# Sums of MLP weights in HBM: begun two to a load in attention, fewer per load behind it

## The chip, the cores and the metric

The kernel runs on one core of one Trainium2 chip. The metric is the device time of one execution in microseconds (us), the median of several runs. One profiled execution stands beside the runs; all rows below come from it.

## The reference

One decoder layer over 512 tokens of width 1024, in float32. A pooling mixer and a sparse attention mixer run side by side on the normed input, are merged by sigmoid gates, go through an output projection, and an MLP with squared ReLU follows. Cut to what matters here:

```python
def reference(x, ...):
    h = rms_norm(x, norm_mix)
    proj = h @ w_in
    y_pool = pool_mixer(u, w_pool, pool_scale)
    y_nsa = nsa_mixer(q, kc, vc, ksl, vsl, kwn, vwn, g_nsa, ...)   # 16 heads, rope on q and k
    merged = g_a * (y_pool @ w_proj_pool) + g_b * (y_nsa @ w_proj_nsa)
    x = x + merged @ w_out
    h = rms_norm(x, norm_mlp)
    x = x + jnp.square(jax.nn.relu(h @ w_ff1)) @ w_ff2
    return rms_norm(x, norm_final)
```

## The kernel before

Every float32 product is made of three faster products: a weight tile is loaded as `raw` (128x1024 floats, 512 KB), ScalarE writes its rounded high part `wh` (lines 304 and 350), VectorE or, in attention, GpSimd for half a tile the rest `wl` (306, 352), and TensorE multiplies high by high, high by low and low by high.

The order of the program is: projections of the input (lines 861 to 894, list `P1`), attention (line 1152, 96 slots; a slot is one block of scores), output projection (`fm3`, `tm3`, from line 1304), MLP (line 1551, four chunks of 1024 hidden channels), final norm. In attention a slot's scores are made on TensorE (`score_pe`), cut and summed by VectorE and ScalarE (`smax`, `expo`), multiplied by their weight two slots later on GpSimd (`weight`, line 1078), turned on TensorE five slots later (`turn_pe`, line 1095) and multiplied with the values (`pv`, 1129). Between the slots TensorE fills in the gate projections of the list `FILL2` (13 weights, `gb0` to `gb7`). The first slots wait for the scores of the compressed branch (`cmp_scores`, 959 to 999): VectorE (971 to 985), GpSimd (`cw`, `PC`, lines 987 to 990), TensorE's turn (996).

The MLP uses a fast matrix multiplication with seven products in place of eight, whose weights are partly sums of quarters of `w_ff1` and `w_ff2`. These sums are made by the DMA engines in HBM, without any compute engine, as 44 jobs in a fixed order. A job `S` has two halves: a copy of one quarter into `S`, issued on SyncE (SP) by `make_sum` (line 263), and an addition of another quarter to `S`, an accumulating DMA issued on GpSimd (POOL) by `add_sum` (line 271). An addition waits until its copy has landed. Some jobs copy another sum (`S2<-S1`, `S4<-S2`), so their copies wait, on SP, until that sum's addition has landed.

When a job is begun is decided by `emit_load` (214 to 239): it puts the next weight load on SP (line 233), asks `sums_after(i)` whether a copy follows load number i, and from load 52 on puts an addition on POOL when more than two jobs are begun. In attention the slot loop puts one addition on POOL behind every fourth slot (lines 1174 and 1175). `make_sum` first puts out additions as long as its source is a sum that has not been added to. Loads are numbered by use: 0 to 34 are `P1`, 35 to 47 `FILL2`, 48 to 55 the nsa projection, 56 to 63 the output projection, from 64 on the MLP. Four `raw` buffers (five later) hold loads, so load i goes out when the weight four before it has been split.

SP also issues four 64 KB copies per rope (`rs<-rx`, line 617), which swap the halves of a head; VectorE's first product of that rope (line 619) overwrites `rx` and waits for them. Instructions of one engine run in the order in which the scheduler of the tile framework puts them, from its own estimate of times; SP and POOL are queues like the others, and an instruction that waits holds all behind it.

Of the kernel before, what the change touches and what calls it, by code (L numbers as in the profile page):

```python
# [62 lines left out]
def trunk(ctx: ExitStack, tc: tile.TileContext, A, out):  # L63
# [41 lines left out]
    def add_key(k):  # L105
# [14 lines left out]
        else:  # L120
# [4 lines left out]
    P1 = ("ck ks u0 wk0 wk1 u1 wk2 u2 kw wk3 cv u3 V0 V1 V2 wv0 q0 wv1 ga0 wv2 wpool q1 wv3 ga1 q5 "  # L125
          "ga2 q2 pp0 q6 pp1 q7 pp2 q3 pp3 q4").split()
    FILL2 = "gb0 gb1 gb2 ga3 gb3 ga4 gb4 ga5 gb5 ga6 gb6 ga7 gb7".split()
# [86 lines left out]
    def emit_load():  # L214

        i = st["load"]
        if i >= len(LD):
            return False
        segs = LD[i]
        a = segs[0][0].shape[1]  # L220
        b = sum(s.shape[2] for s, _ in segs)
        assert a * b <= 1024
        if not by_name() or st["kept"] < RAW:
            st["kept"] += by_name()
            t = wp.tile([128, 1024], F32, tag="raw", bufs=RAW, name=f"raw{i}")
        elif spare:
            t = spare.pop(0)
        else:
            return False
        st["load"] += 1  # L230
        v = t[:, :a * b].rearrange("p (a b) -> p a b", a=a)
        for s, o in segs:
            began = nc.sync.dma_start(v[:, :, o:o + s.shape[2]], s)
        raws[i] = (t, a, b)
        if sums_after(i):
            make_sum(began)
        if i >= len(P1) + len(FILL2) + 4 and (len(begun) > 2 or begun and st["sums"] == len(jobs)):
            add_sum()
        return True

    def sums_after(i):

        if i < MLP0:
            return len(P1) + 3 <= i < len(P1) + len(FILL2) + 8
        return i % 3 == 0

    def by_name():

        return st["load"] >= MLP0

    def give_back(*tiles):
        spare.extend(tiles)
        while spare and by_name() and emit_load():
            pass

    def make_sum(load):

        if st["sums"] < len(jobs):
            to, q, _ = jobs[st["sums"]]
            while any(q is jobs[n][0] for n in begun):  # L260
                add_sum()
            with tc.issue_after(load.ins):
                nc.sync.dma_start(to, q)
            begun.append(st["sums"])
            st["sums"] += 1

    def add_sum(behind=None):

        to, _, q = jobs[begun.popleft()]
        with tc.issue_after(behind.ins) if behind else nullcontext():  # L270
            POOL.dma_start(to, q, accum_op=ALU.add)  # L271
# [15 lines left out]
    def group_steps(i):  # L287

        key, at = WL[i]
        if i in PLUS:  # L290
            while st["load"] <= PLUS[i]:
                assert emit_load()
            t = raws.pop(PLUS[i])[0]
            DVE.tensor_tensor(t, t, held[key], op=ALU.add)
            give_back(held.pop(key))
            yield
        elif isinstance(at, str):
            t = held.pop(key)
        else:
            while st["load"] <= at:  # L300
                assert emit_load()
            t = raws.pop(at)[0]
# [248 lines left out]
    def evac0(i, after=None):  # L551
        sl = slice(128 * i, 128 * i + 128)
        for a in range(2):
            ks = slice(4 * a, 4 * a + 4)
            r = ACT.activation(hT[0][:, ks, sl], trs[i][a], AF.Copy)
            with behind(after) if after else nullcontext():
                v = DVE.tensor_tensor(hT[1][:, ks, sl], trs[i][a], hT[0][:, ks, sl].bitcast(F32), op=ALU.subtract)
        return r, v
# [8 lines left out]
    r, _ = evac0(1)  # L567
# [105 lines left out]
    with ExitStack() as c1:  # L673
# [187 lines left out]
        for k in P1[2:]:  # L861
            i = int(k[-1]) if k[-1].isdigit() else None
# [813 lines left out]
```

## Time and profile before

| | us |
|---|---|
| median of 3 runs (791.01 to 793.32) | 792.94 |
| the profiled execution's own time | 793.79 |
| its span, first to last instruction | 792.0 |
| TensorE busy | 774.8 (98%) |
| VectorE busy | 619.3 (78%) |
| ScalarE busy | 488.6 (62%) |
| GpSimd busy | 179.5 (23%) |
| mean granted TensorE clock | 0.996 of full speed |

A difference to the time before is made against the profiled execution's own time, 793.79, which is 0.85 above the median. Busy TensorE means that a matmul was under way by the profile's modelled ends; a wait of a few tenths of a us can hide in it. DMA rows count 16 engines: a share of 1.00 is all of them busy.

### The profile page before, as it was taken

Reading aid. Unit: us, or ns where it says so; the run is one execution under the profiler, and the core shown is the slowest. Engines: PE = TensorE matmul, PEld = TensorE weight load, DVE = VectorE, ACT = ScalarE, POOL = GpSimd, SP = SyncE. Lnnn points to the kernel's source line nnn. Section 1 sums busy time; section 2 is a strip of 40 time slices with the busy share of each in tenths; the row PEclk is TensorE's granted clock in tenths of the full one; section 3 lists DMA queues with packets and bytes.
Section 4 is the critical chain, followed back from the end, with each engine's and each line's share of the span. In section 5 each row is a group of like instructions: output and inputs, shape, how many; then the busy total and the mean of one; then the engine's idle time right before and its main releaser. Section 6 shows DMA issues by size and latency. Waiting matters only on the chain. (4 is left out here: it accounts for less than half of the span.)

```text
span 792.0 us, 12823 instructions
## 1 busy us (share of the span) xinstructions
PE 774.8 (98%) x4541; PEld 674.1 (85%) x4541; DVE 619.3 (78%) x1177; ACT 488.6 (62%) x962; POOL 179.5 (23%) x245
## 2 busy tenths in 40 slices
PE   8999999999999999999999999999999999999995
PEld 6889877888888888988888899879997999789974
DVE  6888666445999888887656489997899789878897
ACT  6756543335988888896334485934783478247745
POOL 4000000025876666673100000111110110110002
PEclk9999999999999999999999999999999999999998
DMA  9554733487753434335956508989998996978552
GB/s 309 134 152 120 198 108 100 127 213 185 135 108 80 99 90 107 80 81 93 346 145 216 130 1 243 327 205 298 260 289 227 281 285 198 279 227 259 165 181 107
DMA packets 116154, 142.33 MB, mean 180 GB/s; under 512 B 5525, under 2 KB 88121, under 8 KB 115898
## 3 DMA queue, kind: packets, MB, share of 16 engines
q1 hardware_dynamic: 97690, 117.72, 45.8%
q0 software_dynamic: 18112, 23.07, 19.2%
q10 hardware_dynamic: 288, 0.72, 0.3%
q8 instruction: 36, 0.59, 0.3%
q14 instruction: 28, 0.23, 0.1%
HBM read 136.77 MB, written 48.23 MB: 234 GB/s over the span
## 5 line engine op out<-in xcount | busy, mean ns | idle before, releaser
L393 PE MATMUL psF<-R,wh 128*128 128x512 f32 x512 | 164.4, 402 | 0.0
L304 ACT ACTIVATE wh<-raw 128x1024 fp32r<-128x1024 f32 x75 | 79.2, 1058 | 85.7 <-PE psB L1515 32.1
L271 POOL DMA_DIRECT2D S<-w_ff x44 | 48.7, 1107 | 360.3 <-DMA S<-w_ff 286.1
L350 ACT ACTIVATE wh<-raw 128x512 fp32r<-128x512 f32 (+1 forms) x100 | 60.3, 620 | 85.3 <-PE psF L393 43.3
L306 DVE TENSOR_TENSOR wl<-raw,wh 128x1024 fp32r<-128x1024 f32 x75 | 92.2, 1231 | 23.4 <-ACT wh L304 23.4
L393 PEld LDWEIGHTS psF<-R,wh 128*128 128x128 f32 x512 | 92.1, 188 | 17.9
L393 PE MATMUL psF<-R,wl 128*128 128x512 f32 x256 | 101.3, 396 | 0.0
L1078 POOL TENSOR_SCALAR P<-P,sm,GT 128x128 f32<-128x128 f32 (+3 forms) x128 | 83.1, 671 | 55.2 <-DVE sm L1068 38.7
L352 DVE TENSOR_TENSOR wl<-raw,wh 128x512 fp32r<-128x512 f32 (+1 forms) x85 | 58.6, 696 | 26.3 <-ACT wh L350 26.2
L1062 ACT ACTIVATE P<-P,sm 128x128 f32<-128x128 f32 (+3 forms) x128 | 71.1, 559 | 9.9 <-DVE sm L1052 9.2
L1052 DVE CUSTOM_DVE_ANT_0 P<-psS,cst 128x128 f32<-128x128 f32 (+3 forms) x128 | 59.7, 483 | 8.4 <-PE psT L1095 5.3
L1398 PE MATMUL psB<-R,wh 128*128 128x256 f32 x352 | 64.1, 282 | 0.0
L304 ACT ACTIVATE w3h<-raw 128x1024 fp32r<-128x1024 f32 x37 | 39.1, 1055 | 36.3 <-PE psB L1398 14.1
L1110 DVE TENSOR_TENSOR PT<-psT,PT 128x512 fp32r<-128x512 f32 (+2 forms) x96 | 56.6, 596 | 3.5 <-ACT PT L1106 2.9
L393 PEld LDWEIGHTS psF<-R,wl 128*128 128x128 f32 x256 | 48.1, 188 | 11.3
L1106 ACT ACTIVATE PT<-psT 128x512 fp32r<-128x512 f32 (+2 forms) x96 | 49.5, 520 | 8.8 <-PE psT L1095 7.8
L1398 PEld LDWEIGHTS psB<-R,wh 128*128 128x128 f32 x352 | 54.3, 189 | 0.5 <-DVE R L1340 0.2
L306 DVE TENSOR_TENSOR w3l<-raw,w3h 128x1024 fp32r<-128x1024 f32 x37 | 45.8, 1238 | 9.2 <-ACT w3h L304 9.2
L1095 PE MATMUL psT<-ident,P 128*128 128x128 f32 x320 | 50.9, 273 | 0.9 <-DVE PT L1110 0.9
L1398 PE MATMUL psB<-R,wl 128*128 128x256 f32 x176 | 49.5, 281 | 0.0
L1095 PEld LDWEIGHTS psT<-ident,P 128*128 128x128 f32 x320 | 39.4, 140 | 9.7 <-issue 1.8
L1129 PE MATMUL psO<-PT,VV 128*128 128x256 f32 x320 | 47.7, 286 | 0.0
(381 smaller groups left out, 2001.8 us busy)
## 6 DMA issues: line engine op xcount, KB each, us to landing
raw<-w_ff SPq DMA_DIRECT2D x54, 512.0 KB, 6.1
S<-w_ff POOLq DMA_DIRECT2D x44, 512.0 KB, 7.5
raw<-S SPq DMA_DIRECT2D x44, 512.0 KB, 5.0
raw<-w_in SPq DMA_DIRECT2D x32, 512.0 KB, 4.1
S<-w_ff SPq DMA_DIRECT2D x32, 512.0 KB, 7.1
S<-S SPq DMA_DIRECT2D x12, 512.0 KB, 5.3
raw<-w_proj_nsa SPq DMA_DIRECT2D x8, 512.0 KB, 4.4
raw<-w_out SPq DMA_DIRECT2D x8, 512.0 KB, 4.5
```

The costliest lines, as they stand in the source:

```text
L304: ACT.activation(h, t, AF.Copy)
L306: DVE.tensor_tensor(l, t, h.bitcast(F32), op=ALU.subtract)
L350: ACT.activation(h[:, sl], t[:, sl], AF.Copy)
L352: eng.tensor_tensor(l[:, sl], t[:, sl], h[:, sl].bitcast(F32), op=ALU.subtract)
L393: PE.matmul(ps, a, b, start=first and j == 0, stop=last and j == n - 1, skip_group_check=True)
L1052: DVE.tensor_tensor_reduce(out=P[:, o:o + n].rearrange("p (a c) -> p a c", c=128), in0=s, in1=m, scale=1.0, scalar=3e38, op0=ALU.add, op1= ...
L1062: last_exp[:] = [ACT.activation(c, c, AF.Exp, bias=sm[:, 0, e:e + 1], scale=-1.0, accum_out=sm[:, 1, e:e + 1])]
L1078: r = POOL.tensor_scalar(P[:, o:o + n], P[:, o:o + n], sm[:, 2, e:e + 1], GT[:, qb, c + e:c + e + 1], op0=ALU.mult, op1=ALU.mult)
L1095: PE.transpose(pt[:, 128 * j:128 * j + 128], P[:, 128 * j:128 * j + 128], ident)
L1106: ACT.activation(dH, src, AF.Copy)
L1110: DVE.tensor_tensor(dL, src, dH.bitcast(F32), op=ALU.subtract)
L1398: PE.matmul(out, w[u][:, k, 128 * f:128 * f + 128], XB[x][v][:, k, :], **kw)
```

## The change

Copies of sums are begun by another count. Between loads 38 and 47 (attention's filler weights) each load is followed by two copies in place of one; between 48 and 55 (the nsa projection) by one at odd loads in place of one at each; from 64 on (MLP) by one at every fourth load in place of every third. Jobs, their order, and all arithmetic stay. By the end of load 55, 24 jobs are begun where it was 18.

```diff
-        if sums_after(i):
+        for _ in range(sums_after(i)):
             make_sum(began)
...
     def sums_after(i):

+        if i < len(P1) + len(FILL2):
+            return 2 * (i >= len(P1) + 3)
         if i < MLP0:
-            return len(P1) + 3 <= i < len(P1) + len(FILL2) + 8
-        return i % 3 == 0
+            return i % 2 * (i < len(P1) + len(FILL2) + 8)
+        return i % 4 == 0
```

Lines behind 243 carry numbers higher by 2 in the changed kernel.

SP, from load 38 to load 43, the end of the projections and the first slots of attention (`raw38` is the buffer of load 38, `S1_100` the sum S1 of layer 1, chunk 0, group 0). Before:

```order
L233 DMA raw38_1563<-w_in 128x8x128
L263 DMA S1_100_69<-w_ff1 512x1x256
L233 DMA raw39_1613<-w_in 128x8x128
L263 DMA S3_100_70<-w_ff1 512x1x256
L617 DMA rs_348<-rx_347 32x512 x4
L233 DMA raw40_1678<-w_in 128x8x128
L263 DMA S1_101_72<-w_ff1 512x1x256
L233 DMA raw41_1717<-w_in 128x8x128
L263 DMA S3_101_73<-w_ff1 512x1x256
L233 DMA raw42_1755<-w_in 128x8x128
L263 DMA S2_100_71<-S1_100_69 16x8192
L233 DMA raw43_1810<-w_in 128x8x128
```

and in the changed kernel:

```order
L233 DMA raw38_1563<-w_in 128x8x128
L265 DMA S1_100_69<-w_ff1 512x1x256
L265 DMA S3_100_70<-w_ff1 512x1x256
L233 DMA raw39_1614<-w_in 128x8x128
L265 DMA S1_101_72<-w_ff1 512x1x256
L265 DMA S3_101_73<-w_ff1 512x1x256
L619 DMA rs_348<-rx_347 32x512 x4
...
L233 DMA raw42_1762<-w_in 128x8x128
L265 DMA S1_201_77<-w_ff2 256x1x512
L265 DMA S3_201_78<-w_ff2 256x1x512
L233 DMA raw43_1817<-w_in 128x8x128
L265 DMA S1_110_79<-w_ff1 512x1x256
```

Four copies stand ahead of the last rope's `rs<-rx` where two stood, and behind load 42 come the copies of S1_201 and S3_201, which were behind loads 46 and 47.

POOL over the same stretch (`cw` and `PC` belong to the compressed branch of the first pair of heads, `P` is the block of a slot, two slots share a row of `sm`). Before:

```order
L271 DMA S1_100_69<-w_ff1 512x1x256
L352 TENSOR_TENSOR wl36_1665<-raw36_1486,wh36_1664 128x512
L352 TENSOR_TENSOR wl37_1703<-raw37_1530,wh37_1702 128x512
L987 TENSOR_TENSOR cw_1653<-cw_1653,c8_1654 128x8x32
L989 TENSOR_SCALAR PC_136<-cw_1653 128x4x64
L990 TENSOR_TENSOR PC_136<-cw_1653,PC_136 128x4x64
L352 TENSOR_TENSOR wl38_1744<-raw38_1563,wh38_1743 128x512
L352 TENSOR_TENSOR wl39_1787<-raw39_1613,wh39_1786 128x512
L1078 TENSOR_SCALAR P_1797<-P_1797,sm_1796,GT_129 128x128 x2
L1078 TENSOR_SCALAR P_1816<-P_1816,sm_1796,GT_129 128x128 x2
L271 DMA S3_100_70<-w_ff1 512x1x256
L1078 TENSOR_SCALAR P_1832<-P_1832,sm_1831,GT_129 128x256 x2
```

and in the changed kernel:

```order
L989 TENSOR_TENSOR cw_1655<-cw_1655,c8_1656 128x8x32
L354 TENSOR_TENSOR wl38_1751<-raw38_1563,wh38_1750 128x512
L991 TENSOR_SCALAR PC_136<-cw_1655 128x4x64
L992 TENSOR_TENSOR PC_136<-cw_1655,PC_136 128x4x64
L354 TENSOR_TENSOR wl39_1794<-raw39_1614,wh39_1793 128x512
L273 DMA S1_201_77<-w_ff2 256x1x512
L273 DMA S3_201_78<-w_ff2 256x1x512
L1080 TENSOR_SCALAR P_1804<-P_1804,sm_1803,GT_129 128x128 x2
L1080 TENSOR_SCALAR P_1824<-P_1824,sm_1803,GT_129 128x128 x2
L273 DMA S3_101_73<-w_ff1 512x1x256
L273 DMA S1_110_79<-w_ff1 512x1x256
L1080 TENSOR_SCALAR P_1840<-P_1840,sm_1839,GT_129 128x256 x2
```

The split of weight 38 now stands between `cw` and `PC`, and the additions to S1_201 and S3_201 stand ahead of the first slots' weights, those to S3_101 and S1_110 ahead of slot 2. On VectorE the first half of the split of weight 38 (line 352) likewise moved ahead of the last step of `cmp_scores` (line 985).

SP in the last third of the MLP, where the sum S2_230 is copied into S4_230. Before:

```order
L263 DMA S2_230_107<-S3_230_106 16x8192
L233 DMA raw64_4838<-S1_221_97 128x1024
L233 DMA raw66_4886<-S3_220_96 128x1024
L233 DMA raw5_4496<-w_ff2 128x2x512
L263 DMA S4_230_108<-S2_230_107 16x8192
```

and in the changed kernel:

```order
L265 DMA S2_230_107<-S3_230_106 16x8192
L233 DMA raw67_4910<-S2_121_94 128x1024
L233 DMA raw66_4900<-w_ff1 128x4x256
L233 DMA raw64_4850<-w_ff1 128x4x256
L233 DMA raw5_4509<-w_ff2 128x2x512
L265 DMA S4_230_108<-S2_230_107 16x8192
```

Four loads stand between a sum's copy and the copy that needs its addition, where three stood; the pair comes six and five loads earlier.

## Rows read from the trace of the kernel before

**Rows 1.** The page, part 1: busy us, share of the span, instructions.

```profile
PE 774.8 (98%) x4541; PEld 674.1 (85%) x4541; DVE 619.3 (78%) x1177; ACT 488.6 (62%) x962; POOL 179.5 (23%) x245
```

**Rows 2.** Windows by stage: us, busy (instructions) by engine, clock, DMA share, GB/s.

```profile
160.00:190.00 30.00, 30.00 (x139) 24.53 (x138) 13.40 (x29) 12.27 (x27) 9.11 (x8) 1.00 0.76 206
190.00:366.00 176.00, 174.01 (x1138) 153.98 (x1137) 156.84 (x500) 153.71 (x423) 117.64 (x169) 1.00 0.48 100
...
480.00:560.00 80.00, 79.20 (x504) 70.85 (x503) 70.06 (x83) 43.92 (x57) 9.06 (x8) 1.00 0.98 279
560.00:640.00 80.00, 80.00 (x514) 72.30 (x513) 68.92 (x81) 47.14 (x63) 8.94 (x8) 1.00 0.96 264
640.00:720.00 80.00, 78.16 (x497) 70.12 (x496) 67.37 (x80) 44.92 (x59) 7.60 (x8) 1.00 0.84 238
```

**Rows 3.** The page, part 3: DMA queue, packets, MB, share of 16 engines' span.

```profile
q1 hardware_dynamic: 97690, 117.72, 45.8%
q0 software_dynamic: 18112, 23.07, 19.2%
```

**Rows 4.** DMA issues at 120 to 160 us: KB each, median us to landing.

```profile
rs<-rx SPq DMA_DIRECT2D x15, 64.0 KB, 2.0
```

**Rows 5.** DMA issues at 160 to 168 us, same columns.

```profile
S<-w_ff SPq DMA_DIRECT2D x2, 512.0 KB, 5.2
S<-w_ff POOLq DMA_DIRECT2D x1, 512.0 KB, 8.5
```

**Rows 6.** Queues (packets, MB, share) and DMA issues at 169 to 172 us.

```profile
q0 software_dynamic: 328, 0.34, 73.3%
q1 hardware_dynamic: 486, 0.47, 44.3%
...
rs<-rx SPq DMA_DIRECT2D x4, 64.0 KB, 5.1
```

**Rows 7.** Timeline of VectorE: start us, us, line, what [idle before, releaser].

```profile
175.88 0.69 DVE L619 TENSOR_TENSOR rx<-rx,cst 128x512 f32<-128x512 f32 x1 [6.16 <-DMA rs<-rx]
...
182.38 0.17 DVE L985 TENSOR_TENSOR c<-c,GT 128x8 f32<-128x8 f32 x1
182.48 0.69 DVE L352 TENSOR_TENSOR wl<-raw,wh 128x512 fp32r<-128x512 f32 x1
```

**Rows 8.** Timeline of GpSimd, from the compressed branch to slot 3.

```profile
166.63 1.34 POOL L271 DMA_DIRECT2D S<-w_ff  x1 [41.05 <-DMA S<-w_ff]
...
182.67 0.98 POOL L987 TENSOR_TENSOR cw<-cw,c 128x256 f32<-128x256 f32 x1 [4.34 <-ACT GB L912]
...
184.23 0.73 POOL L990 TENSOR_TENSOR PC<-cw,PC 128x256 fp32r<-128x256 f32 x1
184.92 1.30 POOL L352 TENSOR_TENSOR wl<-raw,wh 128x512 fp32r<-128x512 f32 x1
...
190.55 1.75 POOL L1078 TENSOR_SCALAR P<-P,sm,GT 128x128 f32<-128x128 f32 x4 [1.01 <-DVE sm L1068]
192.24 1.13 POOL L271 DMA_DIRECT2D S<-w_ff  x1
194.05 2.60 POOL L1078 TENSOR_SCALAR P<-P,sm,GT 128x256 f32<-128x256 f32 x4 [0.68 <-DVE sm L1068]
```

**Rows 9.** Timeline of TensorE: turns of the compressed branch, of slots 2 and 3.

```profile
186.02 0.46 PE L996 MATMUL psT<-identR,PC 128*128 128x128 f32 x4
...
199.82 0.60 PE L1095 MATMUL psT<-ident,P 128*128 128x128 f32 x4
...
200.85 0.60 PE L1095 MATMUL psT<-ident,P 128*128 128x128 f32 x4
```

**Rows 10.** Timeline of SP's queue: the load of weight 42.

```profile
186.25 0.37 SPq L233 DMA_DIRECT2D raw<-w_in  x1
```

**Rows 11.** Groups by line, GpSimd, 190 to 366 us: busy us, mean ns, idle before.

```profile
L1078 POOL TENSOR_SCALAR P<-P,sm,GT 128x128 f32<-128x128 f32 (+3 forms) x126 | 80.7, 663 | 51.1 <-DVE sm L1068 34.6 <-PE psT L1095 9.7 <-PE psF L393 3.4
L271 POOL DMA_DIRECT2D S<-w_ff x13 | 14.4, 1108 | 0.0
```

**Rows 12.** Waits of SP's queue at 640 to 720 us: us in total, times, longest.

```profile
SPq L263 <- DMA S<-w_ff: 25.0, 3, 9.7
```

**Rows 13.** Timeline of SP's queue in the last third of the MLP.

```profile
669.90 0.47 SPq L263 DMA_DIRECT2D S<-S  x1
670.47 0.52 SPq L233 DMA_DIRECT2D raw<-S  x1
```

**Rows 14.** Timeline of ScalarE, the same stretch.

```profile
675.39 1.06 ACT L304 ACTIVATE wh<-raw 128x1024 fp32r<-128x1024 f32 x1 [1.08 <-DMA raw<-S]
...
685.78 1.06 ACT L304 ACTIVATE wh<-raw 128x1024 fp32r<-128x1024 f32 x1 [4.22 <-DMA raw<-w_ff]
```

**Rows 15.** Waits of TensorE at 676 to 690 us: us in total, times, longest.

```profile
PE psB L1515 <- DVE x L1539: 1.8, 1, 1.8
```

## Prediction

> **What bounds the kernel now.** Read the page's busy line first: TensorE is busy 774.8 of 792.0 us, the others 78% and less [rows 1]. So the time is TensorE's work plus what it waits, and all that any change of transfers can win is 17 us, most of it at the two ends. Then the windows by stage [rows 2]: TensorE has no idle time at 160 to 190 us, 2.0 us in attention (190 to 366), and 0.8, 0.0 and 1.8 us in three stretches of the MLP. DMA is the other column to read there: 0.48 of its 16 engines in attention, 0.98, 0.96 and 0.84 in the MLP. The change moves transfers from the crowded stages to the empty one. What it can win is the MLP's 2.6 us of TensorE waits; what it can lose is any cover in a stage where TensorE does not wait now. Third come the timelines of the stretch in which the moved transfers start [rows 5 to 10]: the reader is to see there how little slack lies between a GpSimd result and the TensorE instruction that takes it.
>
> **Price of a transfer.** POOL's queue holds the 44 additions: 19.2% of 792.0 us is 152 us, 3.5 us of all 16 engines for each. SP's queue moves 117.72 MB in 45.8%, 363 us: 3.1 us per MB, 1.6 us for a copy or load of 0.52 MB [rows 3]. A whole job is 5.1 us. Six jobs leave the MLP: some 30 us of the 222 busy DMA us at 480 to 720.
>
> **Step 1: the compressed branch, 0.8 us lost.** TensorE turns `PC` at 186.02, straight behind a matmul, and `PC` is complete at 184.23 + 0.73 = 184.96 [rows 8, 9]: 1.1 us of slack. The changed order puts the split of weight 38 between `cw` and `PC` on GpSimd, 1.30 us [rows 8], and half of the same split, 0.69 less an overlap of 0.1, ahead of line 985 on VectorE, from which `cw` starts [rows 7, 8]. 1.30 + 0.6 - 1.1 = 0.8 us that TensorE waits. In-order TensorE takes the whole stage along. Ends: 0 (the split on VectorE not ready and no later than before) to 1.3.
>
> **Step 2: the last rope, 3.2 us lost.** The chain of step 1 begins on VectorE behind line 619, which already waits 6.16 us for `rs<-rx` [rows 7]. Earlier ropes land in 2.0 us [rows 4], this one in 5.1 [rows 6], 3.1 more, with one addition under way from 166.63 to 175.1 (8.5 us [rows 5]). In the changed kernel S3_100's copy goes out behind S1_100's, lands 5.2 us later [rows 5], at about 167.5, and its addition follows the first at about 168, before the rope's copies go out at 169.5; S1_101's addition follows at about 172. Two more copies stand ahead on SP. Upper end: two additions and two copies in full, 7.0 + 3.2 = 10.2 us. Lower end: 0, if the copies ahead have drained and engines are shared. I take one addition's worth, 3.2, since the one that was in the way cost 3.1: the nearest row. The 619 chain has no other cover: what it loses, TensorE loses at 186.02. Weight 37's split stands right behind it and moved ahead of line 625, so it stays inside its slack.
>
> The Trainium skill, "DMA: Bandwidth & Descriptors", section "Queues, rings and completion order", says that each DMA engine goes round-robin between queues and changes after a packet. By that rule more additions in line would not hold `rs<-rx` longer than one does now, step 2 would be near 0, and the total near that of the first rival. The 5.1 against 2.0 us of the rope speaks against an even share, though not against any.
>
> **Step 3: the first slots' weights, 1.0 us lost.** Load 42 goes out at 186.25 [rows 10]; the copies of S1_201 and S3_201 now follow it, and their additions stand ahead of the weights of slots 0 and 1, which ran at 190.55 [rows 8]. Shifted by steps 1 and 2, less the 1.1 us by which weight 38 is split earlier, they go out near 189 and land 5.2 to 8.5 us later [rows 5], near 196; two additions of 1.1 us [rows 8] end near 197.5. Then come weights of 1.75, S3_101's addition, S1_110's (its copy is behind load 43, landing near 200), and at 201 the 256-wide weights at 0.65 each, split by the 1.30 us split of weight 40: slot 2 done at 202.3, slot 3 at 205. TensorE turns these at 199.82 and 200.85 now [rows 9], shifted by 4.0: 203.8 and 204.9. That is level. Each us by which the copies land later costs one; ends 0 and 4. I take 1.0, because six more transfers than now are in line in that stretch.
>
> **Step 4: the rest of attention, 0.3 us lost.** Eight more additions of 1.1 us run on POOL until the end of attention, 9 us. They stand behind every fourth slot, on copies begun long before, so none waits. Cover: the weights sit idle 51 us ahead of their instructions [rows 11], and they run some 4 us ahead of their turns [rows 8, 9]. If the cover were gone it would be 1.1 us a time; ends 0 and 1.5. On SP the copies S2_110 and S2_111 find their sums added to or wait a few us with nothing urgent behind.
>
> **Step 5: the MLP, 1.8 us won.** The one TensorE wait of size there is 1.8 us on a VectorE addition [rows 15]. Followed back: ScalarE waits 4.22 us for a load of `w_ff`, after 1.08 us for a load of a sum [rows 14], and that load stood on SP at 670.47 behind the copy S4_230<-S2_230, which held the queue 9.7 us for the addition to S2_230 [rows 12, 13]. With four loads between the pair in place of three and fewer additions in line, the hold shrinks at least by the time to one more load, and its place in the chunk changes. I book the whole 1.8. Ends: 2.6 won (all idle time of the three stretches) and 2 lost (a hold in a worse place). What is late next is VectorE, 70.06 of 80 us busy in the first of these stretches [rows 2]; that stays.
>
> **Sum.** 0.8 + 3.2 + 1.0 + 0.3 - 1.8 = 3.5 us more. Against the profiled 793.79 that is 797.3; the median of the runs lies 0.85 lower, so I forecast **796.4 us**, 0.4% slower.
>
> **Rivals.** A measurement tells about 0.3%, 2.4 us, so "the same" is 790.6 to 795.3.
>
> First: even sharing. If a small copy on SP's queue gets its turn whatever is in line on POOL's, step 2 is 0: 0.8 + 1.0 + 0.3 - 1.8 = +0.3, 793.2 us. For it: at 169 to 172 us both queues move packets, POOL's 0.34 and SP's 0.47 MB [rows 6]. The rule above would give this rival. Against: the rope's 5.1 us. It decides if `rs<-rx` lands no later than 176. Chance 0.28.
>
> Second, on the other side: the MLP was held by its DMA, more than the waits show. If the first slots' copies land before 194 (then steps 2 and 3 are covered), and the relief of 30 DMA us takes all 2.6 us of idle time, 792.9 - 2.6 = 790.3 us, faster. For it: 0.98 and 0.96 DMA share in the MLP. Against: TensorE does not wait at all at 560 to 640 with a share of 0.96 [rows 2]. It decides where step 1's 0.8 is covered too, as by line 985 coming early. Chance 0.17.
>
> Third: the change relieves nothing, because SP's holds only move. Then step 5 is 0 and it is 798.2; with a rope at 5 us late, 800. Inside my forecast's side. A forecast of "slower", with this, has 0.55.
>
> **How the numbers follow.** 0.55 for slower (795.3 to about 801), of which a twentieth may end at 795.3 or less: 0.53 slower, 0.30 the same, 0.17 faster. The range must take in the first rival and the edge of the second: from 790.8. Its upper end is steps 1 to 3 at 1.3 + 5 + 3 with step 5 at 1.8: +7.8, 800.7. Steps 2 and 3 at both full ends at once (10.2 and 4) are left out: they overlap, since what delays TensorE gives the weights time.
>
> **What would show it.** Right: TensorE idle ahead of line 996 (998 in the changed kernel) by 2 to 6 us near 186; VectorE's wait for `rs<-rx` near 9 us; POOL idle ahead of the additions to S1_201 and S3_201; DMA share of 480 to 720 lower by about 0.1; SP's longest wait for a sum below 7 us; no TensorE wait of 1.8 near 687. Wrong: `rs<-rx` landing by 176, the turn at 186 on time, or a TensorE wait over 1 us in a new place of the MLP. A time under 791 would say that steps 1 to 3 together cost nothing.

## The result and the profile after

The changed kernel takes **797.6 us** in the median of five runs (797.07 to 800.41) where the kernel before, run beside it, takes 792.94 (791.01 to 793.68): 4.7 us or 0.6% by the two medians. The ratio formed over all of these runs is 1.0075, with a 95% interval of 1.0050 to 1.0101. So the changed kernel is slower, by 0.6 to 0.75%. The profiled execution took 800.19 us with a span of 798.4, at the upper end of the five; 6.4 us of span have to be found against the 792.0 of before.

The page's busy line and its queues stand as they did [rows 1, 3]:

```profile
PE 776.8 (97%) x4541; PEld 674.3 (84%) x4541; DVE 618.4 (77%) x1177; ACT 489.9 (61%) x962; POOL 178.7 (22%) x245
...
q1 hardware_dynamic: 97690, 117.72, 45.9%
q0 software_dynamic: 18112, 23.07, 19.0%
```

Nothing was added to any engine, so the time is waits, and the windows by stage say where [rows 2]:

```profile
160.00:190.00 30.00, 28.73 (x133) 23.25 (x132) 12.22 (x24) 10.95 (x20) 10.06 (x10) 1.00 1.07 280
190.00:366.00 176.00, 172.35 (x1114) 152.43 (x1113) 152.14 (x493) 150.81 (x416) 122.16 (x173) 0.99 0.60 129
480.00:560.00 80.00, 76.75 (x475) 67.65 (x475) 69.16 (x83) 45.27 (x60) 6.65 (x6) 1.00 0.84 239
560.00:640.00 80.00, 80.00 (x515) 72.31 (x514) 69.19 (x81) 46.81 (x61) 6.73 (x6) 1.00 0.87 241
640.00:720.00 80.00, 79.32 (x507) 71.32 (x506) 68.27 (x81) 46.14 (x61) 6.27 (x6) 1.00 0.81 236
```

The transfers moved as the change says: the DMA share falls from 0.98, 0.96, 0.84 to 0.84, 0.87, 0.81 in the MLP and rises from 0.76 to 1.07 at the end of the projections. TensorE now idles 1.3 us there (0 before) and 3.7 us in attention (2.0), and in the MLP the idle time has moved rather than gone: 3.3, 0.0 and 0.7 us in place of 0.8, 0.0 and 1.8.

The timeline of TensorE shows every wait of attention's start (lines behind 243 have numbers higher by 2):

```profile
187.39 0.54 PE L998 MATMUL psT<-identR,PC 128*128 128x128 f32 x4 [1.27 <-POOL PC L992]
...
202.54 0.96 PE L1097 MATMUL psT<-ident,P 128*128 128x128 f32 x4 [1.13 <-POOL P L1080]
...
205.34 0.69 PE L1097 MATMUL psT<-ident,P 128*128 128x128 f32 x2 [1.03 <-POOL P L1080]
...
223.92 0.30 PE L1097 MATMUL psT<-ident,P 128*128 128x128 f32 x1 [0.34 <-DVE PT L1112]
...
480.79 0.39 PE L1400 MATMUL psB<-xT2H,wh 128*128 128x256 f32 x1 [0.64 <-ACT wh L306]
...
762.91 0.73 PE L1517 MATMUL psB<-w3h,yT2H 128*128 128x512 f32 x2 [0.23 <-ACT w3h L306]
```

The last three rows are waits that the kernel before has too, so they serve as marks. In the timeline of TensorE before they stand at

```profile
218.37 0.30 PE L1095 MATMUL psT<-ident,P 128*128 128x128 f32 x1 [0.32 <-DVE PT L1110]
...
475.50 0.39 PE L1398 MATMUL psB<-xT2H,wh 128*128 128x256 f32 x1 [0.65 <-ACT wh L304]
...
756.42 0.73 PE L1515 MATMUL psB<-w3h,yT2H 128*128 128x512 f32 x2 [0.23 <-ACT w3h L304]
```

With the turn of `PC` (186.02 before [rows 9], 187.39 now) that gives the loss by stretch: **1.4 us** up to that turn; from it to the first mark 36.5 us in place of 32.3, **4.2 us**; from there to the second mark 256.9 in place of 257.1, a gain of 0.3; from the second to the third, the MLP, 282.1 in place of 280.9, **1.2 us**; behind it -0.1. The sum is 6.4.

Of the first: VectorE's wait for the rope is 8.39 us, and the split of weight 38 stands between `cw` and `PC`, as the order said [rows 7, 8]:

```profile
178.04 0.69 DVE L621 TENSOR_TENSOR rx<-rx,cst 128x512 f32<-128x512 f32 x1 [8.39 <-DMA rs<-rx]
```

The timeline of GpSimd over the same stretch and on to the first slots:

```profile
184.30 0.62 POOL L989 TENSOR_TENSOR cw<-cw,c 128x256 f32<-128x256 f32 x1 [6.56 <-DVE c L987]
184.88 1.29 POOL L354 TENSOR_TENSOR wl<-raw,wh 128x512 fp32r<-128x512 f32 x1
...
186.62 0.72 POOL L992 TENSOR_TENSOR PC<-cw,PC 128x256 fp32r<-128x256 f32 x1
...
195.64 2.17 POOL L273 DMA_DIRECT2D S<-w_ff  x2 [5.19 <-DMA S<-w_ff]
197.26 2.29 POOL L1080 TENSOR_SCALAR P<-P,sm,GT 128x128 f32<-128x128 f32 x4
198.97 2.93 POOL L273 DMA_DIRECT2D S<-w_ff  x2
```

Of the second: GpSimd stands 5.19 us in front of two additions whose copies have not landed, and the weights of slots 0 and 1, which ran at 190.55 [rows 8], run at 197.26: 6.7 us later, in a stage that is 1.4 us late up to there.

### The profile page after: what moved, and what is told of

Its sections match the earlier page's. It is cut to its first block, busy times and chain, and to the rows that moved or that the text cites. A ratio compares the mean times of both kernels' runs of the same rounds, so it can differ in the third digit from the quotient of the medians.

```text
span 798.4 us, 12822 instructions
## 1 busy us (share of the span) xinstructions
PE 776.8 (97%) x4541; PEld 674.3 (84%) x4541; DVE 618.4 (77%) x1177; ACT 489.9 (61%) x962; POOL 178.7 (22%) x245
## 5 line engine op out<-in xcount | busy, mean ns | idle before, releaser
L273 POOL DMA_DIRECT2D S<-w_ff x44 | 51.8, 1196 | 365.2 <-DMA S<-w_ff 243.0
L1080 POOL TENSOR_SCALAR P<-P,sm,GT 128x128 f32<-128x128 f32 (+3 forms) x128 | 87.2, 792 | 50.0 <-DVE sm L1070 32.5
```

The lines of the kernel that those rows point to most:

```text
L1080: r = POOL.tensor_scalar(P[:, o:o + n], P[:, o:o + n], sm[:, 2, e:e + 1], GT[:, qb, c + e:c + e + 1], op0=ALU.mult, op1=ALU.mult)
```

## Experiments

"Before" ran beside each group of experiments: its median was 791.95, 792.04 and 791.79 us. The expectations name theories: A, or "theory now", is what the traces had suggested by then; B, the steps of the prediction; C, the prediction's first rival. A ratio is to the kernel before; its 95% interval stands in brackets.

**1. The attention part alone.** The changed kernel, with the MLP's count put back:

```diff
-        return i % 4 == 0
+        return i % 3 == 0
```

> Only the attention part of the change: two copies to a load at loads 38 to 47, odd loads at 48 to 55; the MLP begins one behind every third load, as before. Theory A (read from the changed kernel's trace): the start of attention costs about 5.5 us, 1.4 at the turn of PC near 186 and 4.1 at the first slots' turns at 201 to 204, and the thinned MLP gives nothing that can be counted on, so this kernel lies with the changed one: 798 +- 1 us. Theory B (the prediction's steps): attention costs 5.3 and the MLP gave 1.8 back, so without the thinning the time is 1.8 above the changed kernel's 797.6: about 799.4. Rival C (even sharing of the DMA engines): attention costs 2.1, 795.

Measured: 796.37 us, ratio 1.0056 (1.0040 to 1.0071). That is 4.4 us above before (791.95): less than A (798 +- 1) and B (799.4) said, and 1.4 us more than C's 795. Its TensorE waits for `PC` at 186.59 (0.83 us) and for the weights at 202.69 and 205.47 (1.90, 1.01), and the second mark comes 4.1 us later than before:

```profile
479.61 0.39 PE L1400 MATMUL psB<-xT2H,wh 128*128 128x256 f32 x1 [0.64 <-ACT wh L306]
```

So the loss is in attention. The MLP's thinning, which is the only difference to the change, has won nothing that shows, since the change itself is no faster than this.

**2. Two copies more ahead of the rope, or one addition more.** Two kernels on the kernel before. The first begins 2, 2, 0, 0 copies at loads 38 to 41, and the second addition stays behind slot 1:

```diff
-        if sums_after(i):
+        for _ in range(sums_after(i)):
...
+            if len(P1) + 3 <= i < len(P1) + 7:
+                return 2 * (i < len(P1) + 5)
```

> Before, with the copies of loads 40 and 41 moved up to loads 38 and 39 (2, 2, 0, 0 in place of 1, 1, 1, 1). The second addition stays where it was, behind the weights of slot 1; what is left of the change at the rope is two more copies ahead of rs<-rx on SP and the split of weight 38 between cw and PC on GpSimd. Theory A: rs<-rx lands 0 to 1 us later than the 175.9 of before, since no second addition is in line; the split's 1.3 us against 1.1 us of slack and VectorE's half of the split make TensorE wait 0.5 to 1.5 us at the turn of PC: 793.5 to 794.5. Theory B: 0.8 for the split and up to 1.6 for each copy: 794 to 796. Rival C: the queue is shared evenly and a copy ahead costs nothing: 0.8 at most, 793.7. If the time does not move at all, the split's place costs nothing and the 1.4 us near 186 of the changed kernel is the second addition's.

The second begins 2, 0, 1, 1 and puts both additions in line at load 39, ahead of the rope:

```diff
+        if i == len(P1) + 4:
+            add_sum()
+            add_sum()
...
+            if len(P1) + 3 <= i < len(P1) + 5:
+                return 2 * (i == len(P1) + 3)
```

> Before, with the copy of load 39 moved up behind load 38 and both additions (S1_100, S3_100) in line on GpSimd's queue ahead of the last rope; the copies that stand ahead of rs<-rx on SP are the same two as before, and the split of weight 38 stays behind PC. It measures the second addition by itself. Theory now: the queues are served packet by packet, 102 ns of an addition against 41 of SP's, so SP's queue is slowed as long as any addition is in line, and a second in line does not slow it more; the rope lands within 1 us of before (177 or earlier), the 1.1 us of slack hold, and TensorE turns PC on time: within 0.3% of before. Theory B (the prediction's step 2): the rope lands 3.2 us later, TensorE waits about 2.1 us at the turn of PC: 794. A landing between the two says that what the second addition adds is the time by which it lengthens the slowed stretch.

Measured: 793.91 us, 1.0031 (1.0018 to 1.0045), for the copies; 792.61, 1.0007 (0.9998 to 1.0015), for the addition. VectorE's wait for the rope is nearly the same in both; with the copies it is

```profile
176.81 0.99 DVE L621 TENSOR_TENSOR rx<-rx,cst 128x512 f32<-128x512 f32 x1 [7.64 <-DMA rs<-rx]
```

and with the addition (line 624 there)

```profile
176.82 0.97 DVE L624 TENSOR_TENSOR rx<-rx,cst 128x512 f32<-128x512 f32 x1 [7.66 <-DMA rs<-rx]
```

So either one cost the rope 1.5 us in its one profile (6.16 before [rows 7]), half of the 3.2 that the prediction booked. With the copies TensorE waits 0.83 us at the turn of `PC`, with the addition not at all: there the split of weight 38 stays behind `PC`, the way from the rope to the end of `PC` takes 8.4 us where it took 9.1, and the slack takes the rest. With both, the wait is 7.62 in experiment 1, 8.39 and 9.11 in two executions of the changed kernel, and 10.21 in experiment 3, whose order is the same up to there: 1.5 to 4.1 us more than before, 2.7 in the mean. One execution does not give this size to better than a us or two.

**3. The forced additions.** A copy of a sum forces out, ahead of itself, the additions that its source still lacks. In the changed kernel, such an addition is now kept behind the weights last given out:

```diff
             while any(q is jobs[n][0] for n in begun):
-                add_sum()
+                add_sum(st.get("last"))
...
-                last = weight(i - 2)
+                st["last"] = last = weight(i - 2)
```

> The changed kernel, with the additions that a copy of a sum forces (those to S1_201, S3_201 and S1_110) kept behind the weights of the slot last given out, so that they no longer stand on GpSimd ahead of the weights of slots 0 to 3. Theory A: the 4 us of TensorE waits at 201 to 206 go, the 1.3 at 187 stays: 793.5 to 794.5. Theory B: only 1.0 goes: 796.6. Rival: the three additions now stand ahead of the second pair's cw and the SP queue is held longer for S2_110: the loss moves to 220 to 250 us and the time stays at 797 to 798.

Measured: 796.73 us (792.91 to 800.58), 1.0057 (1.0038 to 1.0076). The waits for `P` are gone:

```profile
189.28 0.54 PE L998 MATMUL psT<-identR,PC 128*128 128x128 f32 x4 [2.43 <-POOL PC L992]
...
221.96 0.30 PE L1097 MATMUL psT<-ident,P 128*128 128x128 f32 x1 [0.30 <-DVE PT L1112]
```

From the turn of `PC` to the first mark it takes 32.7 us (32.3 before, 36.5 in the change), so the 4 us are these additions. The time did not follow, and the 794 of theory A is missed. B's number, 796.6, is met, but by luck: B had only 1.0 us go here. In the profiled execution the rope was later still:

```profile
179.50 0.69 DVE L621 TENSOR_TENSOR rx<-rx,cst 128x512 f32<-128x512 f32 x1 [10.21 <-DMA rs<-rx]
```

with 2.43 us of wait at the turn of `PC`, 0.8 for a weight ahead of it, and later 0.28 and 0.59 at the second pair's `PC` and at a score. Up to the rope both programs have one order, so the 10.21 against 8.39 is a difference between executions; the waits at 235 to 245 us, 0.9 in all, are the smaller part. The runs of this kernel spread over 7.7 us, more than those of any other here.

**4. Pairs from load 40.** The change, with one copy each at loads 38 and 39:

```diff
-            return 2 * (i >= len(P1) + 3)
+            return (i >= len(P1) + 3) + (i >= len(P1) + 5)
```

> The changed kernel with loads 38 and 39 followed by one copy each, as before, and pairs from load 40 on (22 jobs begun by load 55). The two copies that stood ahead of the last rope are gone, the split of weight 38 stands behind PC again, and the additions that a copy of a sum forces no longer stand ahead of the weights of slots 0 to 3. Theory now: the whole loss of the change is these two places; TensorE turns PC on time, the waits at 201 to 205 are gone, and the time is within 0.3% of before, 791 to 793.5 (the thinned MLP giving between 0 and 1). Rival: eight more copies and additions at 172 to 250 us load the queue all the same and attention loses 2 us or more in other places: 794 to 796, as the kernel with pairs at loads 48 to 53 did.

Measured: 791.66 us (790.55 to 792.84), ratio 0.9996 (0.9987 to 1.0005). Two copies fewer at loads 38 and 39, and the whole loss is gone. The split stands behind `PC` again, the rope is no longer what VectorE's line 621 waits for, and GpSimd comes to the weights of slots 0 and 1 at the time of before (190.55 [rows 8]):

```profile
175.62 0.69 DVE L621 TENSOR_TENSOR rx<-rx,cst 128x512 f32<-128x512 f32 x1 [5.73 <-ACT wh L352]
...
190.72 1.74 POOL L1080 TENSOR_SCALAR P<-P,sm,GT 128x128 f32<-128x128 f32 x4 [1.01 <-DVE sm L1070]
```

The DMA share of 160 to 190 us is 1.00 all the same (0.76 before [rows 2], 1.07 in the change), and 22 jobs are begun by load 55, where the change begins 24. So what the change lost it lost by which transfers stand ahead of two results, and hardly by how much is moved.

**5. The MLP without its additions.** The kernel before, with the additions of the 26 jobs that are begun in the MLP left out:

```diff
+        job = begun.popleft()
+        if job >= 18:
+            return
```

> Before, with the additions of the 26 jobs that are begun in the MLP left out (their copies stay): the MLP then multiplies with plain copies in place of these sums. It bounds what any thinning of the sums in the MLP can win. Theory now: TensorE's waits there come from a few meetings of a load with an addition and are 1 to 2 us in a middling run, so this kernel is 1 to 2 us faster than before: 790 to 791. Theory B (the prediction's step 5): 1.8 to 2.6 us, 789.4 to 790.1. Rival: transfers hold the MLP more than its waits show; then 4 us or more. If it is within 0.3% of before and the waits at 516 and 756 remain, nothing was to be had from the MLP's sums at all.

Measured: 790.63 us (790.06 to 791.02), ratio 0.9982 (0.9973 to 0.9991): 1.4 us. The DMA share of the three stretches falls to 0.67, 0.64 and 0.60, and of TensorE's waits there one is left:

```profile
PE psB L1518 <- DVE yT3L L1456: 0.5, 1, 0.5
```

All 26 additions together are worth 1.4 us in the median, so six fewer could not be counted on for 1.8.

**6. Both kernels profiled a second time.** No edit.

> The kernel before, unchanged, for a second profile of it. The profiled run of before took 793.79 us where the median of the runs beside the last experiments was 791.95. Theory now: the TensorE wait of 1.8 us at 687, on which the prediction's step 5 stands, is a matter of which transfer met which in that one execution: it is gone or under 1.0 us here, and the MLP from the first matmul of its up projection near 474 us to the same instruction near 756 us is shorter than 281.3 by 1 to 2 us. Theory B (the prediction): the hold of SP for S2_230 is part of the order of the program, so the 1.8 us wait stands at 687 again.

> The changed kernel, unchanged, for a second profile of it. Theory now: the loss at the start of attention is here again, 4.5 to 5.5 us between 186 and 275 us, in two parts, near 187 and at 201 to 205; the TensorE waits of 0.9, 0.6 and 1.1 us at 498, 522 and 535 are of the one execution, and at least one of them is gone: the MLP's stretch of 282.5 us comes out at 279.5 to 281.5. Rival: the thinned order itself makes these waits; then they stand here again at the same instructions, and the stretch is 282.5.

Measured: 793.91 and 796.30 us. In the kernel before, the 1.8 us at 687 are not there; a wait of 0.9 for the same operation stands in the stretch 560 to 640, where TensorE had not waited at all:

```profile
PE psB L1515 <- DVE x L1539: 0.9, 1, 0.9
```

SP's hold for the addition to a sum, from which the prediction had derived the 1.8, stands as it did, at 640 to 720 us and with the same longest wait (9.7 [rows 12]):

```profile
SPq L263 <- DMA S<-w_ff: 21.6, 3, 9.8
```

It is 9.7 and 9.5 in the two kernels of experiment 2, where the wait at that operation is 0.45 and 0.46 us, and 9.8 in experiment 1, where there is none. So the hold by itself does not make the wait.

In the changed kernel the waits at 498, 522 and 536 are all gone, and that at 695 too; one of 0.5 us, which both kernels have, stays. Attention's loss is there again, with other shares:

```profile
188.05 0.75 PE L998 MATMUL psT<-identR,PC 128*128 128x128 f32 x4 [2.43 <-POOL PC L992]
...
206.32 0.44 PE L1097 MATMUL psT<-ident,P 128*128 128x128 f32 x2 [1.02 <-POOL P L1080]
```

The MLP from the second mark to the third is, with every third load, 280.9 and 279.9 (before twice), 280.5 and 279.2 (experiment 2) and 279.4 (experiment 1): 280.0 in the mean. With every fourth it is 282.1 and 278.5 (the change twice), 279.0 (3), 280.0 (4), 279.7 and 280.1 (7): 279.9. Without additions it is 278.2. The pace makes no difference that eleven profiles show.

**7. Pairs late in attention.** The thinned MLP, with single copies up to load 47 and pairs at loads 48 to 53, against the kernel before; profiled twice.

```diff
+            late = i - len(P1) - len(FILL2)
+            return (1 + (0 <= late < 6)) * (len(P1) + 3 <= i and late < 8)
...
+        return i % 4 == 0
```

> The thinned MLP without the early pairs: one copy to a load at 38 to 47 as before, two at 48 to 53, one at 54 and 55 (24 begun by load 55, as in the changed kernel), every fourth load in the MLP. Theory A: nothing is lost near 186 and 201 to 204, and the MLP gains between 0 and 1 us: 792 to 793, within 0.2% of before. Theory B: the MLP's 1.8 us come: 791.1. Rival: six copies and additions more between loads 48 and 53 hold attention's weights there as they did at its start: 1 to 3 us more than before, 794 to 796, with TensorE waits on P between 220 and 330 us.

> The kernel with pairs at loads 48 to 53, unchanged, for a second profile: its first profile was its fastest run (793.53 of 793.5 to 796.4) and showed only 1 us more TensorE waits than before, at 354 to 366 us. Theory now: the pairs of loads 52 and 53 bring a burst of additions near the end of attention and the waits at 354 to 366 are larger here, 2 to 3 us. Rival: the loss is not there but in the MLP, where a wait of 1 us or more stands in a new place.

Measured: 795.11 us (793.53 to 796.43), 1.0036 (1.0022 to 1.0050), and 797.91 in the execution of the second profile. The time is the rival's, 794 to 796. Nothing is lost near 186 to 205, and yet it is slower: the mechanism of the first slots stands at the end of attention, later than the 220 to 330 us that the rival named. The waits of GpSimd at 330 to 366 us in the second profile:

```profile
POOL S L272 <- DMA S<-S: 6.8, 1, 6.8
POOL S L272 <- DMA S<-w_ff: 3.5, 1, 3.5
```

Before, GpSimd waits for no transfer there. TensorE then waits 2.6 us for VectorE's `PT` and 0.7 for `P` at 300 to 372 us, 0.3 and nothing before. That the waits for `PT` hang on the same additions is argued from their places, behind GpSimd's, and not shown by a run. The rival's MLP wait is there too (1.21 us at 613.90), in a stretch whose sum is no longer than before.

## Why the prediction came out right, and which of its steps did not

The forecast of 796.4 us and the measured 797.6 lie 1.2 us apart, with the sign and the range right. Steps 1 to 4 were booked at 5.3 us, and 5.3 us is what the profiled execution lost up to the second mark. That this agrees to a tenth is luck: `PC` cost 2.6 us less than steps 1 and 2 had booked, the first slots 3.2 more and the rest of attention 0.6 less, and the profiled execution is one of the two slowest of five. And step 5 is wrong.

- **Step 1, the compressed branch: 1.9 booked, less 1.1 of slack; 0.2 found.** From the start of VectorE's rope line to the end of `PC` it was 9.08 us before (175.88 to 184.96) and is 9.30 now (178.04 to 187.34), though the 1.29 us split stands between `cw` and `PC`. Most of it came back on VectorE, where line 625 (627 now) took 1.67 us beside a split on GpSimd and takes 0.68 now:

```profile
177.20 1.67 DVE L625 TENSOR_TENSOR oT<-rx,rs 128x512 f32<-128x512 f32 x1
...
179.85 0.68 DVE L627 TENSOR_TENSOR oT<-rx,rs 128x512 f32<-128x512 f32 x1
```

- **Step 2, the last rope: 3.2 booked, 2.2 in the trace, 1.5 for one cause alone.** The mechanism is right, and over four executions of this order (1.5, 2.2, 3.0 and 4.1) the size is too. The row it was priced by does not carry it: "one addition's worth" put the whole on the second addition, and in experiment 2 that costs 1.5 us, as the two copies do, which the step left at nothing. Steps 1 and 2 together gave 0.2 + 2.2 less the slack of 1.1, and TensorE waited 1.27 us where 4.0 were booked.
- **Step 3, the first slots' weights: 1.0 booked, 4.2 found.** The largest error. The step named the right additions, and its reckoning of 197.5 for their end is near: the weights run at 197.26. So are its 202.3 and 205 for the weights of slots 2 and 3: TensorE turns them at 202.54 and 205.34, straight behind its waits. What it got wrong is the cover: it took TensorE to come to them at 203.8 and 204.9, behind 4.0 us of loss at `PC`. Since `PC` cost only 1.4, TensorE came 2.6 us earlier and waited for the same weights. Steps 2 and 3 share one delay, as the range's last sentence said of their ends, and to that extent the sum held for a reason. The second profile (experiment 6) bears this out: there `PC` cost more and the slots less, and the first mark comes at 223.69, as here (223.92). Of the 4.2 us, 2.2 are the two waits, 1.1 is lost behind the second wait, at the lowered clock of 204 to 208 us (below), and 0.4 is the turn of slot 2 itself, which takes 0.96 us where it took 0.60 [rows 9]; the rest is not put down to a row.
- **Step 4: a loss of 0.3 booked, 0.3 won.** Next to nothing either way.
- **Step 5, the MLP: 1.8 won was booked, nothing was won.** This step failed, and in its first sentence: a wait of one execution was taken for a property of the program. The hold behind it did shrink as told (SP's longest wait for a sum is 4.7 us, 9.7 before [rows 12]), but experiment 6 shows the wait at 687 gone without any change, with the hold at 9.8, and experiment 5 that all additions cost 1.4. So the step from the hold to TensorE's wait is wrong too, not only its size. The profiled 793.79 of before also lies above the median of 791.9 that later runs gave.

The new waits of 0.46 to 0.90 us at 498 to 536, which the changed kernel's first profile has and its second has not, fit a meeting of a load with an addition. In the first, an addition was issued at 488.37 and a load of `w_ff` at 488.41, and ScalarE waited 3.94 us for the load. In the kernel before, that load went out at 483.12, the addition behind it, at 483.72, and ScalarE waited 0.92. In the second profile of the changed kernel the load went out at 488.18, the addition at 489.31, and ScalarE, at 497.35, waited for TensorE and not for the load. The wait of 0.46, at 522, has its like in the second profile of the kernel before (0.40 at 517), so it is not the change's. That this order is the cause is argued, not shown.

Of the rivals, even sharing was right for part of the time only. In the changed kernel the queues at 172 to 182 us are

```profile
q0 software_dynamic: 1384, 1.38, 87.1%
q1 hardware_dynamic: 1072, 0.76, 31.8%
```

1.3 packets of an addition to one of SP's queue, at 101 and 47 ns each (0.871 and 0.318 of 160 engine-us, over the packets). The Trainium skill, "DMA: Bandwidth & Descriptors", section "Queues, rings and completion order", has the engines go round-robin by packet. At 176 to 180 us this trace agrees with it, if the profile's packets are the skill's:

```profile
q0 software_dynamic: 549, 0.55, 84.4%
q1 hardware_dynamic: 535, 0.29, 35.1%
```

In the stretch right behind the issue of the rope's copies the turns are not equal. In the kernel before, these copies were issued from 169.50 on, and at 171 to 172 us, of these two queues, only the addition's moved anything. With two additions in line (the second kernel of experiment 2) the copies were issued from 168.95 on, and at 169 to 173 the additions moved all packets but one, although earlier ropes had landed 2.0 us after their issue [rows 4]. First before, then that kernel:

```profile
q0 software_dynamic: 187, 0.19, 120.2%
...
q0 software_dynamic: 695, 0.70, 115.8%
q1 hardware_dynamic: 1, 0.00, 0.2%
```

Rows 6, which the prediction read for this rival, are an average over such stretches: SP's 486 packets there had all moved by 171. Why the rope's copies stand back no run shows. So a cost near 0 did not follow from sharing. The rope's copies stand back at first, and where the turns are equal, packets twice as long leave SP's queue 0.07 MB/us (0.29 MB in 4 us), where the prediction's price from [rows 3] is 1.6 us for 0.52 MB. A second addition in line lengthens this stretch: at 173 to 175 us SP's queue moved 131 packets with it, and 688 before.

The signs named in the prediction: the rope's wait near 9 (8.39), GpSimd idle ahead of the additions (5.19), the MLP's share lower by about 0.1, SP's holds below 7 (4.7) and no 1.8 near 687 (0.68) came. The wait of 2 to 6 us near 186 came in the second profile only (2.43; 1.27 in the first). The missing 1.8 tells nothing about step 5: without the change, too, it was gone in a second profile.

## What to carry to other kernels

Before work is moved into a stage with idle DMA engines, ask not how much room there is but which small result is awaited behind the moved transfers, on the same queue and on the engine that issues their additions; in this change two copies at loads 38 and 39 make the difference between 0.75% and nothing, with nearly the same traffic in the stage. A wait for a transfer that one profile shows is a wait of that execution until a second profile shows it; leave the suspected work out once, and its whole price is known before any of it is moved. Read the shares of two queues in stretches as short as the transfer in question: an average over 3 or 10 us can show sharing where one queue stood still. And where two steps delay the same chain, the later one's cover must be reckoned with the earlier one's cost at both of its ends.

## What the runs showed of the hardware that was not expected

A TensorE wait can cost more than itself. In the second profile of the changed kernel TensorE waited 2.43 us at the turn of `PC`, and the windows behind it show the granted clock (the third figure from the end) at 0.50, the lower of its two levels, 1.2 GHz:

```profile
186.00:188.00 2.00, 0.00 (x0) 0.00 (x0) 0.79 (x1) 0.59 (x2) 1.91 (x3) 0.99 1.46 529
188.00:190.00 2.00, 1.95 (x7) 1.67 (x8) 0.00 (x0) 1.12 (x2) 0.00 (x0) 0.50 0.64 188
190.00:192.00 2.00, 2.00 (x9) 1.70 (x8) 0.22 (x3) 0.00 (x0) 1.28 (x1) 0.65 0.84 223
```

A matmul of 128x512 takes 0.63 us there and 0.39 at full clock. In the first profile the 1.27 us at `PC` left the clock at 1.00, and it fell behind the waits for `P`: 0.67 at 204 to 206 and 0.50 at 206 to 208 us. In experiment 1, waits of 0.83, 1.90 and 1.01 us left it at 1.00 throughout. In experiment 3 a wait as long as that of the second profile, 2.43 us at the same turn, which ended at 189.28, left it at 1.00 too:

```profile
190.00:192.00 2.00, 2.00 (x12) 1.74 (x11) 0.45 (x5) 1.09 (x3) 0.95 (x1) 1.00 1.02 304
```

So the length of a wait alone does not tell whether the clock falls.

GpSimd's records get longer beside a run of additions: the first three weights of 128x256 take 2.97 us at 200.56 in the changed kernel, where four took 2.60 at 194.05 before [rows 8], and the split of a weight 2.60 at 202.16 where it takes 1.30. That does not show slower work, because the records overlap: the split starts at 202.16, the weights ahead of it end at 203.53. From 195.64 to 212.26 us, 16.6 us with next to no idle time, GpSimd issued six additions and did fourteen weights, a split and a `cw`; the mean times of before for these, at 190 to 207 us, add up to 17.8. Beside a run of additions it counts when the next result is ready, not how long a record is.
